# A two-layer encoder's 256-token matmul stages: the high weights take the high and the low activations in one 512-column matmul

## The chip, the cores and the metric

One core of one Trainium2 chip. The metric is the time of one execution on the device in microseconds (us), the median of three runs. PE is the matrix engine (TensorE), PEld its weight load, DVE the vector engine, ACT the scalar engine, POOL the GpSimd engine, SP the engine whose queue issues nearly all loads.

## The reference

Two layers of an encoder, each a mixer and a SwiGLU feed-forward network (FFN), each of these wrapped as x <- LayerNorm(alpha x + f(x)). Layer 0 mixes with a diagonal state space and latent attention, layer 1 with a Mamba-2 scan. All is float32. In front of the 256 tokens stand 16 meta tokens; their positions are dropped at the end, so from the z part of layer 1's mixer on only 256 tokens are needed.

```python
D_MODEL = 2048
BATCH = 1
SEQ = 256
...
def mamba2_mixer(h, w_in, conv_w, conv_b, dt_bias, a_log, d, norm_g, w_out):
    bsz, n, _ = h.shape
    zxbcdt = h @ w_in
    z = zxbcdt[..., :SSD_INNER]
...
    y = y.reshape(bsz, n, SSD_INNER) * jax.nn.silu(z)
...
    return y @ w_out

def swiglu_ffn(h, w_gate, w_up, w_down):
    return (jax.nn.silu(h @ w_gate) * (h @ w_up)) @ w_down
```

## The kernel before, in words

Activations lie with features on partitions and tokens on columns. Every matrix product goes through `linear` (L135): it walks a list SEQ[name] of weight tiles (m, k) of 128 x 128, row tile m after row tile m, and adds the products over k into one PSUM tile of 512 float32 columns (one bank) per m. Float32 is kept by splitting: a weight tile is high + low, an activation tile high + low, each part in the type float32r, and three matmuls (L162 to L164) make high x high, high weights x low activations and low weights x high activations, all into the same 256 or 272 columns. The high and the low activations are two tiles (hh and hl for a layer's input, ah and al for the FFN's hidden features, yh and yl for the output of the scan).

The weights come in loads of eight tiles on SP's queue (L121, four buffers). ACT casts a load to its high part (L126) and DVE subtracts (L127) to make the low part; three buffers hold the pairs. In the input projection and the output projections of layer 1 both work in halves of 512 columns. When the last k of a row tile is done, `evac` reads PSUM: in the FFN silu on ACT for a gate tile (m < 44), a product on DVE for an up tile, then a split; in the down product an addition to x on DVE; for z (m < 32 of the input projection) silu on ACT; in the output projection an addition to x on DVE. Four PSUM tiles take turns as accumulators in these stages.

The stages of layer 1 with 256 tokens: the z tiles of the input projection (in1_0 to in1_7, which the trace calls mm_in; between them stand tiles with 272 tokens for the scan), the output projection in three parts (out1a, out1b, out1c: 16, 8 and 8 tiles k for each of the 16 m), and the FFN (gate and up in gu_a and gu_b, down in dn_a and dn_b; here with a 1 behind the name for layer 1, which the trace leaves out and whose input it calls m1hh, m1hl). In out1c and dn_b `ln_add` (L282) adds the last part to x and goes on to the sums of the layer norm; gu_a1 takes its first seven row tiles before the norm is known, with two more columns (258), and corrects them afterwards.

A scheduler that simulates the program sets the order of the instructions on each engine; each engine then runs its list strictly in order.

Of the kernel before, what the change touches and what calls it, by code (L numbers as in the profile page):

```python
# [8 lines left out]
F32 = mybir.dt.float32  # L9
F32R = mybir.dt.float32r  # L10
# [8 lines left out]
N = 272          # tokens with the meta tokens  # L19
NM = 16          # meta tokens  # L20
NS = 256         # tokens without them
D = 2048
DT = 16          # feature tiles of the model width
KC = 8           # weight tiles per load
# [4 lines left out]
NHT = 44         # hidden tiles of the FFN  # L29
HH = 22          # hidden tiles of one half  # L30


# ---------------------------------------------------------------- orders
def seq_rows(ms, ks, first=0):
    """Order of the weight tiles (m, k): the first `first` row tiles interleaved
    over k, the others one after the other."""
    s = [(m, k) for k in ks for m in ms[:first]]
    for m in ms[first:]:
        s += [(m, k) for k in ks]
    return s  # L40


# the tiles after a layer norm, in the order in which its results come
KS = list(range(8, 16)) + list(range(8))
PRE = (3, 1, 1, 2)  # groups of the row tiles that take the sums before the norm
# [41 lines left out]
# vectors by feature: name -> (first column, columns)  # L87
# [12 lines left out]
# ---------------------------------------------------------------- kernel  # L100
class Trunk:
# [9 lines left out]
    # ---- weights: load, split exactly into two parts of 12 bits each  # L111
# [23 lines left out]
    def linear(self, name, rhs, evac, n, pre=None):  # L135
        """rhs(k, m) -> (hi, lo) [128, n]; n may be a function of m. pre: (norm, tile), with
        the first row tiles taken before the norm and corrected after it."""
# [9 lines left out]
        for i, (m, k) in enumerate(seq):  # L147
# [6 lines left out]
            if m in before:  # L154
                nn += 2
                o = ps[m][:, :nn]
                xh, xl = rhs(k, m, 2)
            else:
                xh, xl = rhs(k, m)
            st = left[m] == tot[m]  # L160
            left[m] -= 1
            nc.tensor.matmul(o, lhsT=wh, rhs=xh, start=st, stop=False)  # L162
            nc.tensor.matmul(o, lhsT=wh, rhs=xl, start=False, stop=False)  # L163
            nc.tensor.matmul(o, lhsT=wl, rhs=xh, start=False, stop=left[m] == 0)  # L164
            if left[m] == 0:
                del ps[m]
# [16 lines left out]

    def split(self, hi, lo, src):
# [3 lines left out]
    # ---- sums over features, token by token: (tokens of a tile) on partitions, tiles on columns  # L188
# [4 lines left out]
    def colsum(self, o, terms, ones, n):  # L193
        """o [tokens, tiles] = sum over partitions of the terms [128, n], times the value of ones"""
# [8 lines left out]
    def spread(self, pool, ps, r, n):  # L203
        """r [tokens, tiles] to all partitions, [128, n] in PSUM"""
# [10 lines left out]
    def rsqrt(self, pool, v, n, act, e=None):  # L215
        """1 / sqrt(v), v [tokens, tiles] in SBUF, >= eps > 0; Newton steps after a first guess"""
# [21 lines left out]
    def rms(self, pool, ps, sq, w, n, e=None):  # L238
        """1 / sqrt(mean of squares + eps), to all partitions in PSUM; sq: sums of squares by partition"""
# [12 lines left out]
    # ---- layer norm over features (partitions and tiles), token by token.  # L252
    # x is kept as x - K, K the mean over the first feature tile, and the sums are taken of that.
    # Up to the first row tiles of the next matrix W, g (x - K) goes for the result:
    #   W (g (x - mean) r + b) = r (W g (x - K)) - (mean - K) r (W g) + W b,
    # with g and b as two more columns.
    def ln_begin(self, pool, ps, xs, g=None, b=None, hh=None, hl=None, late=0, tag=None):
        n = xs[0].shape[-1]
        if hh is not None:
            for j, v in ((N, g), (N + 1, b)):  # L260
                v = self.vecs[:, VEC[v][0]:VEC[v][0] + DT]
                self.split(hh[:, :, j], hl[:, :, j], v)
        return dict(pool=pool, ps=ps, xs=xs, n=n, g=g, b=b, hh=hh, hl=hl, late=late, tag=tag)
# [1083 lines left out]
```

## Time and profile before

| | |
|---|---|
| time, median of 3 runs | 2723.07 us (2720.76 to 2724.64) |
| span of the profiled execution | 2719.2 us |
| PE busy | 2654.8 us (98%), 21808 matmuls |
| DVE busy | 1680.2 us (62%) |
| ACT busy | 1275.6 us (47%) |
| POOL busy | 421.6 us (16%) |
| loads | mean 171 GB/s |

The span runs from the first to the last instruction of the one profiled execution; the timed runs are other executions of the same program, and what they take beyond the span lies before its first instruction and after its last. Busy times are averages over stages with different limits. PE's records are pipelined and overlap, so its busy share says that something is always in it, and the distance from one start to the next says how fast it goes. In layer 1, gu_a1 begins at 1929 us, dn_a1 at 2191, gu_b1 at 2318 and dn_b1 at 2569; out1a lies from 1619 to 1709, out1b from 1820 to 1879 and out1c from 1879 to 1929.

### The profile page before, as it was taken

To read this page: it belongs to the slowest core of one execution; us is meant where nothing else is said; L and a number is where in the kernel's file an instruction comes from. 1 tells how busy PE (TensorE), PEld (TensorE's weight loads), DVE (VectorE), ACT (ScalarE), POOL (GpSimd) and SP (SyncE) were. 2 spreads that over 40 slices of the span, in tenths; PEclk is the share of its full clock that TensorE was granted. 3 is DMA by queue.
4 is the path that set the end of the run, shared out by engine and by line. 5 is a ranking of instruction groups with operands and counts; after the bars stand their busy time and mean duration, and the time that the engine had idled before them with its cause. 6 is when DMAs were issued, how large, how long until landed. Compare 5 with 4: busy or idle time off the path is not lost.

```text
span 2719.2 us, 52890 instructions
## 1 busy us (share of the span) xinstructions
PE 2654.8 (98%) x21808; PEld 2600.5 (96%) x21808; DVE 1680.2 (62%) x2692; ACT 1275.6 (47%) x2040; POOL 421.6 (16%) x576
## 2 busy tenths in 40 slices
PE   9899999999999999999999999999899999999997
PEld 8677999999999999999999999999899999999997
DVE  7768587444444445669677775788964444444555
ACT  5545456333333334447555554555654433444443
POOL 5844061000000001220001110113500000000042
PEclk9899999999999999999999999999999999999999
DMA  7233545555555555545655555554556556565663
GB/s 244 84 109 103 187 155 158 176 171 176 175 177 172 175 174 172 178 151 180 209 158 191 179 175 189 173 162 144 187 189 183 184 185 184 183 185 185 186 180 116
DMA packets 139682, 465.30 MB, mean 171 GB/s; under 512 B 14832, under 2 KB 30000, under 8 KB 139312
## 3 DMA queue, kind: packets, MB, share of 16 engines
q1 hardware_dynamic: 139296, 461.71, 54.5%
q8 instruction: 171, 2.80, 0.4%
q14 instruction: 71, 0.58, 0.1%
q10 hardware_dynamic: 144, 0.21, 0.0%
HBM read 458.58 MB, written 3.28 MB: 170 GB/s over the span
## 4 chain that ended last, share of the span: by engine, by line
PE 88%; DVE 6%; POOL 3%; issue 1%; ACT 1%; DMA 1%; SPq 0%; DVEq 0%; ACTq 0%; POOLq 0%
PE mm_gu_b L164 6%; PE mm_gu_b L163 6%; PE mm_gu_b L162 6%; PE mm_gu_a L164 6%; PE mm_gu_a L162 6%; PE mm_gu_a L163 6%; PE mm_in L163 5%; PE mm_in L162 5%; PE mm_in L164 5%; PE mm_dn_b L162 3%; PE mm_dn_a L162 3%; PE mm_dn_b L164 3%; PE mm_dn_b L163 3%; PE mm_dn_a L164 3%; PE mm_dn_a L163 3%
## 5 line engine op out<-in xcount | busy, mean ns | idle before, releaser
L127 DVE TENSOR_TENSOR lo_gu_b<-st_gu_b,hi_gu_b 128x1024 fp32r<-128x1024 f32 x176 | 215.7, 1226 | 235.6 <-ACT hi_gu_b L126 235.6
L127 DVE TENSOR_TENSOR lo_gu_a<-st_gu_a,hi_gu_a 128x1024 fp32r<-128x1024 f32 x176 | 216.3, 1230 | 188.3 <-ACT hi_gu_a L126 186.8
L126 ACT CAST hi_gu_b<-st_gu_b 128x1024 fp32r<-128x1024 f32 x176 | 184.9, 1050 | 308.5 <-PE mm_gu_b L163 226.6
L126 ACT CAST hi_gu_a<-st_gu_a 128x1024 fp32r<-128x1024 f32 x176 | 184.4, 1048 | 251.4 <-PE mm_gu_a L163 190.4
L163 PE MATMUL mm_in<-f0hl,hi_in 128*128 128x256 f32 (+1 forms) x1024 | 293.2, 287 | 0.0
L162 PE MATMUL mm_in<-f0hh,hi_in 128*128 128x256 f32 (+1 forms) x1024 | 292.6, 286 | 0.0
L164 PE MATMUL mm_in<-f0hh,lo_in 128*128 128x256 f32 (+1 forms) x1024 | 292.5, 286 | 0.0
L304 POOL TENSOR_TENSOR x<-x,ln_k 128x272 f32<-128x272 f32 (+1 forms) x56 | 60.1, 1111 | 1396.6 <-ACT ln_k L302 1298.2
L127 DVE TENSOR_TENSOR lo_in<-st_in,hi_in 128x512 fp32r<-128x512 f32 (+1 forms) x268 | 183.4, 716 | 96.4 <-ACT hi_in L126 95.6
L126 ACT CAST hi_in<-st_in 128x512 fp32r<-128x512 f32 (+1 forms) x268 | 158.3, 636 | 148.0 <-PE mm_in L163 135.3
L164 PE MATMUL mm_gu_a<-mixhh,lo_gu_a 128*128 128x272 f32 (+1 forms) x704 | 203.7, 291 | 3.5 <-DVE lo_gu_a L127 3.5
L162 PE MATMUL mm_gu_a<-mixhh,hi_gu_a 128*128 128x272 f32 (+1 forms) x704 | 204.0, 290 | 1.1 <-DVE fix L276 1.1
L163 PE MATMUL mm_gu_a<-mixhl,hi_gu_a 128*128 128x272 f32 (+1 forms) x704 | 204.3, 291 | 0.0
L163 PE MATMUL mm_gu_b<-mixhl,hi_gu_b 128*128 128x272 f32 x704 | 203.5, 289 | 0.0
L164 PE MATMUL mm_gu_b<-mixhh,lo_gu_b 128*128 128x272 f32 x704 | 203.5, 289 | 0.0
L162 PE MATMUL mm_gu_b<-mixhh,hi_gu_b 128*128 128x272 f32 x704 | 203.4, 289 | 0.0
L164 PE MATMUL mm_gu_a<-m1hh,lo_gu_a 128*128 128x256 f32 (+1 forms) x704 | 198.5, 283 | 4.9 <-DVE lo_gu_a L127 4.9
L162 PE MATMUL mm_dn_b<-ah,hi_dn_b 128*128 128x272 f32 (+1 forms) x704 | 201.1, 286 | 0.0
L164 PE MATMUL mm_dn_b<-ah,lo_dn_b 128*128 128x272 f32 (+1 forms) x704 | 201.1, 286 | 0.0
L163 PE MATMUL mm_dn_b<-al,hi_dn_b 128*128 128x272 f32 (+1 forms) x704 | 201.0, 286 | 0.0
L162 PE MATMUL mm_dn_a<-ah,hi_dn_a 128*128 128x272 f32 (+1 forms) x704 | 201.0, 286 | 0.0
L164 PE MATMUL mm_dn_a<-ah,lo_dn_a 128*128 128x272 f32 (+1 forms) x704 | 200.9, 285 | 0.0
(519 smaller groups left out, 8886.4 us busy)
## 6 DMA issues: line engine op xcount, KB each, us to landing
st_gu_a<-in_w_gu_a SPq DMA_DIRECT2D x176, 512.0 KB, 3.6
st_gu_b<-in_w_gu_b SPq DMA_DIRECT2D x176, 512.0 KB, 3.6
st_in<-in_w_in SPq DMA_DIRECT2D x140, 512.0 KB, 3.7
st_dn_a<-in_w_dn_a SPq DMA_DIRECT2D x88, 512.0 KB, 3.5
st_dn_b<-in_w_dn_b SPq DMA_DIRECT2D x88, 512.0 KB, 3.5
st_in1h<-in_w_in1h SPq DMA_DIRECT2D x34, 512.0 KB, 3.6
st_out1a<-in_w_out1a SPq DMA_DIRECT2D x32, 512.0 KB, 3.6
st_out0b<-in_w_out0b SPq DMA_DIRECT2D x16, 512.0 KB, 3.9
```

The costliest lines, as they stand in the source:

```text
L126: nc.scalar.copy(hi[:, j:j + w], st[:, j:j + w])
L127: nc.vector.tensor_tensor(lo[:, j:j + w], st[:, j:j + w], hi[:, j:j + w], op=ALU.subtract)
L162: nc.tensor.matmul(o, lhsT=wh, rhs=xh, start=st, stop=False)
L163: nc.tensor.matmul(o, lhsT=wh, rhs=xl, start=False, stop=False)
L164: nc.tensor.matmul(o, lhsT=wl, rhs=xh, start=False, stop=left[m] == 0)
L304: (nc.vector if j < 2 else nc.gpsimd).tensor_tensor(xs[j], xs[j], st["k"], op=ALU.subtract)
```

## The change

High and low activations of a tile lie in one tile now, side by side ([128, k, 2, tokens]: hx, ax, yx). Where a matmul has exactly 256 columns, `linear` sends the high weights against both halves in one instruction of 2 x 256 columns, which fills the 512 columns of the PSUM tile; the low weights go against the high half and into the first 256 columns as before. A row tile thus ends as two partial sums, p and q, which `evac` adds: where silu or a product follows, a new helper `merged` copies q with ACT and adds p with DVE; where x is added to, DVE adds p and then q. Products with 258, 260, 272 or 274 columns keep their three matmuls. The FFN's silu tiles get a fifth buffer. The operands of layer 0 get the same layout. All else in the diff is names and removed comments.

```diff
...
             if m in before:
                 nn += 2
                 o = ps[m][:, :nn]
-                xh, xl = rhs(k, m, 2)
+                x2 = rhs(k, m, 2)
             else:
-                xh, xl = rhs(k, m)
+                x2 = rhs(k, m)
+            xh, xl = x2[:, 0, :], x2[:, 1, :]
             st = left[m] == tot[m]
             left[m] -= 1
-            nc.tensor.matmul(o, lhsT=wh, rhs=xh, start=st, stop=False)
-            nc.tensor.matmul(o, lhsT=wh, rhs=xl, start=False, stop=False)
-            nc.tensor.matmul(o, lhsT=wl, rhs=xh, start=False, stop=left[m] == 0)
+            if nn == NS:
+                nc.tensor.matmul(ps[m].rearrange("p (a b) -> p a b", a=2), lhsT=wh, rhs=x2, start=st, stop=False)
+                nc.tensor.matmul(o, lhsT=wl, rhs=xh, start=False, stop=left[m] == 0)
+            else:
+                nc.tensor.matmul(o, lhsT=wh, rhs=xh, start=st, stop=False)
+                nc.tensor.matmul(o, lhsT=wh, rhs=xl, start=False, stop=False)
+                nc.tensor.matmul(o, lhsT=wl, rhs=xh, start=False, stop=left[m] == 0)
             if left[m] == 0:
-                del ps[m]
+                t = ps.pop(m)
+                if nn == NS:
+                    evac(m, o, t[:, NS:])
+                    continue
                 if m not in before:
                     evac(m, o)
                     continue
...
                 if not groups:
                     self.ln_split(pre[0])
 
+    def merged(self, t, p, q):
+        if q is None:
+            return p
+        self.nc.scalar.copy(t, q)
+        self.nc.vector.tensor_tensor(t, t, p, op=ALU.add)
+        return t
...
-    def ln_add(self, st, i, p):
+    def ln_add(self, st, i, p, q=None):
         nc, pool, n, xs = self.nc, st["pool"], st["n"], st["xs"]
         x = xs[i]
-        nc.vector.tensor_tensor(x, x, p, op=ALU.add)
+        for a in (p, q):
+            if a is not None:
+                nc.vector.tensor_tensor(x, x, a, op=ALU.add)
         self.ln_sums(st, i, x)
...
     def operand(self, name):
-        return (self.res.tile([P, DT, N + 2], F32R, tag=t, name=name + t) for t in ("hh", "hl"))
+        return self.res.tile([P, DT, 2, N + 2], F32R, tag="hx", name=name)
...
             for half in range(2):
-                ah = pool.tile([P, HH, n], F32R, tag="ah", name=f"ah{layer}{half}")
-                al = pool.tile([P, HH, n], F32R, tag="al", name=f"al{layer}{half}")
+                ax = pool.tile([P, HH, 2, n], F32R, tag="ax", name=f"ax{layer}{half}")
                 hold = {}
 
-                def evac(m, p):
+                def evac(m, p, q=None):
+                    s = pool.tile([P, n], F32, tag="silu", bufs=5, name="silu")
                     if m < NHT:
-                        s = hold[m] = pool.tile([P, n], F32, tag="silu", bufs=4, name="silu")
-                        nc.scalar.activation(s, p, AF.Silu)
+                        hold[m] = s
+                        nc.scalar.activation(s, self.merged(s, p, q), AF.Silu)
                         return
                     j = m - NHT
+                    p = self.merged(s, p, q)
                     s = hold.pop(j)
                     nc.vector.tensor_tensor(s, s, p, op=ALU.mult)
-                    self.split(ah[:, j - half * HH, :], al[:, j - half * HH, :], s)
+                    self.split(ax[:, j - half * HH, 0, :], ax[:, j - half * HH, 1, :], s)
 
...
                 def rhs_d(k, m):
-                    return ah[:, k - half * HH, :], al[:, k - half * HH, :]
-                def evac_d(m, p):
+                    return ax[:, k - half * HH, :, :]
+                def evac_d(m, p, q=None):
                     if half == 0:
                         nc.vector.scalar_tensor_tensor(xs[m], xs[m], ALPHA, p, op0=ALU.mult, op1=ALU.add)
+                        if q is not None:
+                            nc.vector.tensor_tensor(xs[m], xs[m], q, op=ALU.add)
                     else:
-                        self.ln_add(st2, m, p)
+                        self.ln_add(st2, m, p, q)
...
             def proj(g):
-                def evac(m, p):
+                def evac(m, p, q=None):
                     if m < 32:
                         z = pool.tile([P, NS], F32, tag="z", bufs=8, name="z")
-                        nc.scalar.activation(z, p, AF.Silu)
+                        nc.scalar.activation(z, self.merged(z, p, q), AF.Silu)
                         z_t[m] = z
...
             def wout(name, ks, first, final):
-                def evac(m, p):
+                def evac(m, p, q):
+                    if final:
+                        self.ln_add(st, m, p, q)
+                        return
                     if first:
                         nc.vector.scalar_tensor_tensor(xl[m], xl[m], ALPHA, p, op0=ALU.mult, op1=ALU.add)
-                    elif final:
-                        self.ln_add(st, m, p)
                     else:
                         nc.vector.tensor_tensor(xl[m], xl[m], p, op=ALU.add)
+                    nc.vector.tensor_tensor(xl[m], xl[m], q, op=ALU.add)
 
                 def yr(k, m):
-                    yh, yl = ys[k // 4]
-                    return yh[:, k % 4, :], yl[:, k % 4, :]
+                    return ys[k // 4][:, k % 4]
...
+        yx = ys[g] = pool.tile([P, 4, 2, NS], F32R, tag="yx", bufs=4, name="yx")
         r = self.rms(pool, ps, [tot], 512, NS, nc.gpsimd)
         for j in range(4):
             nc.vector.scalar_tensor_tensor(yf[j], yf[j], self.vec("ssd_g", 4 * g + j), r, op0=ALU.mult, op1=ALU.mult)
-            self.split(yh[:, j, :], yl[:, j, :], yf[j])
+            self.split(yx[:, j, 0, :], yx[:, j, 1, :], yf[j])
```

The scheduler's order on DVE at three places. First, the end of the input projection (the z tiles 28 to 31 of in1_7) and the first weights of out1b; lo_x is the low part of a load, mm_x the accumulator. Before:

```order
L186 TENSOR_TENSOR yl<-z,yh 128x256 x4
L127 TENSOR_TENSOR lo_in_7_13_21193<-st_in_7_13_21190,hi_in_7_13_21192 128x512 x2
L127 TENSOR_TENSOR lo_in_7_14_21227<-st_in_7_14_21224,hi_in_7_14_21226 128x512 x2
L127 TENSOR_TENSOR lo_in_7_15_21260<-st_in_7_15_21257,hi_in_7_15_21259 128x512 x2
L127 TENSOR_TENSOR lo_out1b_21596<-st_out1b_21593,hi_out1b_21595 128x512 x2
```

and now:

```order
L198 TENSOR_TENSOR z<-z,mm_in_7_28_20432 128x256
L127 TENSOR_TENSOR lo_in_7_14_20586<-st_in_7_14_20583,hi_in_7_14_20585 128x512 x2
L198 TENSOR_TENSOR z<-z,mm_in_7_29_20485 128x256
L127 TENSOR_TENSOR lo_in_7_15_20611<-st_in_7_15_20608,hi_in_7_15_20610 128x512 x2
L127 TENSOR_TENSOR lo_out1b_20939<-st_out1b_20936,hi_out1b_20938 128x512 x2
L198 TENSOR_TENSOR z<-z,mm_in_7_30_20538 128x256
```

Each z tile's accumulator is now read by DVE between two splits. Second, the beginning of out1b, ahead of a long run of scan work (y, z, de). Before:

```order
L809 TENSOR_TENSOR x_3477<-x_3477,mm_out1b_21601 128x256
L127 TENSOR_TENSOR lo_out1b_21698<-st_out1b_21695,hi_out1b_21697 128x512 x2
L809 TENSOR_TENSOR x_3477<-x_3477,mm_out1b_21635 128x256
L127 TENSOR_TENSOR lo_out1b_21732<-st_out1b_21729,hi_out1b_21731 128x512 x2
L925 SCALAR_TENSOR_TENSOR y<-xs,vecs,y_p 128x256 x2
```

and now:

```order
L831 TENSOR_TENSOR x_3475<-x_3475,mm_out1b_20944 128x256
L127 TENSOR_TENSOR lo_out1b_21020<-st_out1b_21017,hi_out1b_21019 128x512 x2
L831 TENSOR_TENSOR x_3475<-x_3475,mm_out1b_20971 128x256
L127 TENSOR_TENSOR lo_out1b_21047<-st_out1b_21044,hi_out1b_21046 128x512 x2
L832 TENSOR_TENSOR x_3475<-x_3475,mm_out1b_20944 128x256
L832 TENSOR_TENSOR x_3475<-x_3475,mm_out1b_20971 128x256
```

The second halves of the first two row tiles (L832) stand behind two more loads' splits and ahead of the scan's y. Third, the middle of out1c, where m1hl (now m) is the next matrix's operand, ln_s the sums of the norm. Before:

```order
L269 SCALAR_TENSOR_TENSOR m1hl<-x_3477,vecs,m1hh 128x256
L285 TENSOR_TENSOR x_3477<-x_3477,mm_out1c_22450 128x256
L313 TENSOR_TENSOR ln_s_22180<-ln_s_22180,x_3477 128x256
L127 TENSOR_TENSOR lo_out1c_22565<-st_out1c_22562,hi_out1c_22564 128x512 x2
L269 SCALAR_TENSOR_TENSOR m1hl<-x_3477,vecs,m1hh 128x256
L313 TENSOR_TENSOR ln_s_22180<-ln_s_22180,x_3477 128x256
L285 TENSOR_TENSOR x_3477<-x_3477,mm_out1c_22490 128x256
L127 TENSOR_TENSOR lo_out1c_22605<-st_out1c_22602,hi_out1c_22604 128x512 x2
```

and now:

```order
L304 TENSOR_TENSOR x_3475<-x_3475,mm_out1c_21631 128x256
L286 SCALAR_TENSOR_TENSOR m_21368<-x_3475,vecs,m_21368 128x256
L304 TENSOR_TENSOR x_3475<-x_3475,mm_out1c_21664 128x256
L127 TENSOR_TENSOR lo_out1c_21758<-st_out1c_21755,hi_out1c_21757 128x512 x2
L332 TENSOR_TENSOR ln_s_21403<-ln_s_21403,x_3475 128x256
L304 TENSOR_TENSOR x_3475<-x_3475,mm_out1c_21664 128x256
L286 SCALAR_TENSOR_TENSOR m_21368<-x_3475,vecs,m_21368 128x256
L304 TENSOR_TENSOR x_3475<-x_3475,mm_out1c_21697 128x256
L127 TENSOR_TENSOR lo_out1c_21791<-st_out1c_21788,hi_out1c_21790 128x512 x2
L304 TENSOR_TENSOR x_3475<-x_3475,mm_out1c_21697 128x256
```

Every row tile has two additions from its accumulator (L304) where it had one (L285), with a split or a sum between them.

## Rows read from the trace of the kernel before

**Rows 1.** The page, its head and part 1: busy time by engine.

```profile
span 2719.2 us, 52890 instructions
...
PE 2654.8 (98%) x21808; PEld 2600.5 (96%) x21808; DVE 1680.2 (62%) x2692; ACT 1275.6 (47%) x2040; POOL 421.6 (16%) x576
```

**Rows 2.** The page, part 4: chain that ended last, by engine.

```profile
PE 88%; DVE 6%; POOL 3%; issue 1%; ACT 1%; DMA 1%; SPq 0%; DVEq 0%; ACTq 0%; POOLq 0%
```

**Rows 3.** Windows: us, then busy us (records) of PE, PEld, DVE, ACT, POOL; clock; DMA; GB/s.

```profile
2400.00:2500.00 100.00, 100.00 (x843) 100.00 (x843) 49.36 (x53) 41.73 (x52) 0.00 (x0) 1.00 0.60 184
2210.00:2310.00 100.00, 100.00 (x836) 100.00 (x835) 46.91 (x47) 36.30 (x35) 0.00 (x0) 1.00 0.60 183
...
1630.00:1700.00 70.00, 70.00 (x599) 70.00 (x599) 37.84 (x63) 28.54 (x50) 0.00 (x0) 1.00 0.60 189
900.00:1000.00 100.00, 100.00 (x792) 100.00 (x792) 46.61 (x50) 39.58 (x49) 0.00 (x0) 1.00 0.55 173
680.00:780.00 100.00, 100.00 (x801) 100.00 (x800) 45.81 (x47) 34.67 (x33) 0.00 (x0) 1.00 0.58 175
```

**Rows 4.** Timeline of PE at the vp matmuls (start, us), and vp among the groups by form.

```profile
121.51 1.88 PE L607 MATMUL vp<-wv,kvl 128*80 128x512 f32 x4
...
L607 PE MATMUL vp<-wv,kvl 128*128 128x512 f32 x8 | 3.6, 592 | 0.0
```

**Rows 5.** Groups by line and form, PE, whole span: xcount | busy us, mean ns.

```profile
L164 PE MATMUL mm_gu_b<-m1hh,lo_gu_b 128*128 128x256 f32 x704 | 198.2, 282 | 0.0
...
L164 PE MATMUL mm_gu_a<-m1hh,lo_gu_a 128*128 128x256 f32 x592 | 166.4, 282 | 0.0
...
L164 PE MATMUL mm_in<-f0hh,lo_in 128*128 128x256 f32 x512 | 145.4, 284 | 0.0
...
L164 PE MATMUL mm_dn_a<-ah,lo_dn_a 128*128 128x256 f32 x352 | 99.6, 283 | 0.0
...
L164 PE MATMUL mm_out1a<-yh,lo_out1a 128*128 128x256 f32 x256 | 71.6, 280 | 0.0
...
L164 PE MATMUL mm_out1b<-yh,lo_out1b 128*128 128x256 f32 x128 | 36.1, 285 | 0.0
```

**Rows 6.** Groups by line, ACT, 1879 to 1930 us.

```profile
L302 ACT COPY ln_k<-ln_kp 128x256 f32<-128x256 f32 x1 | 0.4, 362 | 0.0
```

**Rows 7.** What PE waited for, 1800 us to the end: us in total, times, longest us.

```profile
PE mm_gu_a L164 <- DVE lo_gu_a L127: 4.9, 3, 3.1
PE mm_out1c L164 <- DVE lo_out1c L127: 2.3, 4, 1.0
```

**Rows 8.** Timelines of DVE and PE in out1b and out1c: start us, us, instruction, [idle before].

```profile
1840.35 0.40 DVE L809 TENSOR_TENSOR x<-x,mm_out1b 128x256 f32<-128x256 f32 x1
1840.67 0.68 DVE L127 TENSOR_TENSOR lo_out1b<-st_out1b,hi_out1b 128x512 fp32r<-128x512 f32 x1
...
1841.64 0.28 PE L164 MATMUL mm_out1b<-yh,lo_out1b 128*128 128x256 f32 x1
...
1917.78 0.38 PE L164 MATMUL mm_out1c<-yh,lo_out1c 128*128 128x256 f32 x1 [0.97 <-DVE lo_out1c L127]
```

**Rows 9.** Windows, as rows 3: input projection, gu_b1, then out1b and out1c in four pieces.

```profile
1305.80:1618.80 313.00, 312.81 (x2594) 304.74 (x2593) 230.07 (x490) 174.36 (x326) 34.22 (x60) 1.00 0.57 181
...
2317.90:2569.00 251.10, 251.10 (x2113) 251.10 (x2113) 124.18 (x131) 105.00 (x131) 0.00 (x0) 1.00 0.59 185
...
1820.20:1841.40 21.20, 21.20 (x190) 19.27 (x189) 20.36 (x55) 10.42 (x17) 3.16 (x3) 1.00 0.25 77
1841.40:1879.20 37.80, 37.19 (x326) 35.64 (x325) 32.83 (x70) 16.41 (x34) 9.58 (x27) 1.00 0.55 168
1879.20:1900.20 21.00, 20.54 (x172) 20.29 (x171) 17.48 (x30) 11.84 (x26) 10.98 (x12) 1.00 0.45 151
1900.20:1930.20 30.00, 27.48 (x216) 26.00 (x216) 29.69 (x43) 16.70 (x35) 22.35 (x22) 1.00 0.50 157
```

**Rows 10.** Timeline of DVE at the end of dn_b1.

```profile
2698.19 0.42 DVE L285 TENSOR_TENSOR x<-x,mm_dn_b 128x256 f32<-128x256 f32 x1 [7.79 <-PE mm_dn_b L164]
```

## What I expected of the change, before it ran

> **What bounds the kernel now.** I read the engine table first: PE is busy 2654.8 of 2719.2 us and DVE 1680.2 [rows 1]; then the chain of work that ended last, which runs 88% on PE and 6% on DVE [rows 2]. So the time is, nearly everywhere, the matmul count times the spacing of matmuls. A busy PE is not a PE at its peak, so the next view is that spacing: windows that lie wholly inside one stage, with the number of PE records [rows 3]. A record lasts 0.28 us (0.29 at 272 columns; [rows 5]) and they start about 0.12 us apart, so some 2.4 (2.3) of the counted ones began before the window. In the 256-token stages this gives 100 us / 840.6 = 118.9 ns (gate/up), 100 / 833.6 = 120.0 ns (down) and 70 / 596.6 = 117.3 ns (out1a); in the 272-token stages 100 / 789.7 = 126.6 ns and 100 / 798.7 = 125.2 ns. The granted clock is 1.00 in all five, the upper level of 2.4 GHz. At one column per clock 256 columns are 106.7 ns and 272 are 113.3 ns. So every matmul carries 12.2, 13.3, 10.7, 13.3 and 11.9 ns beyond its columns. What the change is worth hangs on whom this excess belongs to: the instruction or its columns.
>
> **Whose the excess is.** If it were the columns', 16 more of them would add 256 to 272 in proportion: 7.4 to 7.5 ns. Gate/up adds 126.6 - 118.9 = 7.7, down adds 125.2 - 120.0 = 5.2; the mean, 6.4, is 0.40 ns a column, beside 0.417 at 2.4 GHz. So the two pairs together say: per instruction, about 12 ns; the gate/up pair alone would say: per column. Sixteen columns are a short lever, and I keep both readings. A third reading comes from the only 512-column matmuls, vp in plain float32 [rows 4]: four records take 1.88 us, a record is 0.59 long, so three spacings of 0.429 us, which is twice 512 columns (426.7 ns) and under 3 ns more. They take a column in two clocks, so they don't show what a fast long matmul pays, only that a long slow one pays almost nothing.
>
> The Trainium skill speaks against the change here: TensorE: Matmul & The Clock Gate, section "Back-to-back issue gap", gives N / 2.4 + 2.5 ns for an N-column matmul, and its Part 2 says that loading the next weights takes no read bandwidth from the running one. This case's spacing of 118.9 ns stands 9.7 ns over that formula's 109.2. By the formula alone a merged pair would save 2.5 ns and the whole change 3024 x 2.5 = 7.6 us; by the rows it is 10.7 to 13.3 each.
>
> **The change part by part.** (1) *Matmuls.* Each weight tile of a 256-column stage goes from 256 + 256 + 256 columns in three instructions to 512 + 256 in two, with one weight load fewer. The tiles are 704 in gu_b1, 592 in gu_a1 (its first seven row tiles stay at 258 columns and three instructions), 352 each in dn_a1 and dn_b1, 512 in the z part of the input projection, 256 in out1a, 128 each in out1b and out1c [rows 5]. If the excess is the instruction's, one excess goes per tile: gate/up 1296 x 12.2 = 15.8 us, z 512 x 12.2 = 6.2 (the same operand layout; taken from gate/up, since z alternates with 272-column tiles), down 704 x 13.3 = 9.4, out1a 256 x 10.7 = 2.7. Sum 34.1 us. Out1b and out1c would give another 256 x 11 = 2.8, which I count as nothing, for the reason in (3).
>
> (2) *ACT.* 113 more copies of the low half (81 silu, 32 z). The nearest row is the copy of 128x256 out of PSUM, 0.36 us [rows 6]. In gu_b1 that is 44 x 0.36 = 16 us on an engine busy 105 of 251; no price. The banks are held longer, but four take turns and one row tile lasts 16 x 0.36 = 5.7 us; the list of what PE waits for between 1800 us and the end has no eviction in it; its two longest lines are the splits [rows 7].
>
> (3) *DVE.* 193 more additions of 128x256, one operand in PSUM: 44 + 37 silu, 32 z, 16 in each of dn_a1, dn_b1, out1a, out1b, out1c. The row is the addition of x in out1b: 0.40 us long, and the next instruction starts 0.32 after it [rows 8]. In gu_b1 DVE goes from 124 to 124 + 44 x 0.40 = 142 us of a stage of 242 [rows 9]: covered. Out1a and the two down stages stay under two thirds [rows 3]. In the input projection DVE is busy 230 of 313 us [rows 9] and gets 20 x 0.40 = 8 more: covered by the mean, with a rival below. The cover is gone from out1b to the first gate/up tiles. Four windows that follow on each other [rows 9] show DVE busy 20.36 of 21.2, 32.83 of 37.8, 17.48 of 21.0 and 29.69 of 30.0 us. At 1841.64 PE starts on a low half whose split ended 0.3 us before, at 1840.67 + 0.68; and from 1900 it starts each low half when the split releases it, as at 1917.78 after 0.97 us idle [rows 8]. Step by step, from the order: before the split at 1841.35 stand six new additions (the z tiles 28 to 31, two of out1b): 6 x 0.32 = 1.9, less the lead of 0.3, a stall of 1.6 us. Between there and 1900 stand 18 (14 of out1b, 4 of out1c): 5.8 to 7.2 us against 8.5 us in which DVE was idle in the two windows (37.8 - 32.8 and 21.0 - 17.5); I take 0, and 5.8 as the upper bound. From 1900 to 1930 ten, with no idle time: 3.2 to 4.0, I take 3.6. Behind the first gate/up split two, 0.6 us: PE is waiting for these very splits (4.9 us in three waits [rows 7]). Sum 5.8 us, bounds 4 to 12. A PE that is faster there only waits longer, hence the zero in (1). ACT, which casts the high half ahead of each split, is busy 45 of these 89 us (16.4 + 11.8 + 16.7) and is not what comes next.
>
> (4) *The end.* The last row tile of dn_b1 has two dependent additions where it had one of 0.42 us, alone on the path [rows 10]: 0.4 us.
>
> (5) *No price:* the operands' new layout moves no instruction, SP issues the same loads (907 rows of order before and now), and the first layer has the same matmuls, with 272 columns throughout.
>
> Sum: -34.1 + 5.8 + 0.4 = -27.9 us on the span of 2719.2. The median of the three runs is 2723.07, so 3.9 us lie around the span. 2719.2 - 27.9 + 3.9 = 2695.2 us.
>
> **The rivals.** *A. The excess is the columns'.* For it: the gate/up pair (7.7 ns for 16 columns); against it: the down pair (5.2). Then 512 columns cost as two times 256, nothing is saved, and only the price of DVE's additions from 1841 us on is left, with the end: +6.2 us, 2719.2 + 6.2 + 3.9 = 2729.3, slower. It decides as soon as a merged pair saves under 6.2 us / 2768 tiles = 2.2 ns. *A'.* The same, but a small part is the instruction's, the 2.7 ns that vp shows over its columns: 2768 x 2.7 = 7.5 us back, 2721.8, no change. It would be the outcome by the formula of the Trainium skill named above (TensorE: Matmul & The Clock Gate). *B. A long matmul hides what a short one pays,* as vp does: then the 512-column one keeps 2.7 ns of its excess too. Further gain: (1296 + 512) x 9.5 + 704 x 10.6 + 256 x 8.0 = 26.7 us, 2668.5. Against it: vp runs at half the rate. *C. DVE's queue holds the splits up.* The additions wait for a copy on ACT, which waits for PE's last matmul of the row tile, and behind them on DVE stand the splits of the next weights. In the z parts that can cost 8 groups x about 1 us: 2703.2. Against it: DVE is idle a quarter of that stretch, and PE waits for no split there. *D. It doesn't do what it says:* excluded by the order: in these stages, and in no others, a 512- and a 256-column matmul stand where three of 256 stood, 3024 instructions fewer.
>
> **How the numbers follow.** Forecast 0.66, with bounds of its own from 10.7 to 13.3 ns a tile (29.6 to 36.8 us) and 4 to 12 us on DVE: 2690 to 2706. B 0.10, C 0.08, A' 0.07, A 0.09. Faster by over 0.2%, about what a measurement here can tell from no change (5.4 us), holds for the forecast, B and C: 0.84; within 0.2% is A', 0.07; slower is A, 0.09. The range takes in the forecast, C and A' (0.81) and part of the way to B: 2680 to 2724.
>
> **What would show it.** In gu_b1 a weight tile, now 3 x 118.9 = 357 ns, takes 344.5 by the forecast, 334.9 by B, about 354 by A' and 357 by A; in dn_a1 346.7 instead of 360. From 1841 on, shifted by what was saved earlier, the list of PE's waits should hold lo_out1b, lo_out1c and lo_gu_a with some 14 us together instead of 7, and DVE should be busy over 95% in out1c. If PE's waits are no longer there, step (3) is wrong; if the tile time is not near 344, step (1).

## The result: 2707.4 us, and the profile after

| | before | after |
|---|---|---|
| median (range), us | 2723.2 (2720.8 to 2724.6) | 2707.4 (2705.9 to 2710.2) |
| ratio to before | | 0.9939, 95% interval 0.9922 to 0.9956 |
| span of the profiled execution, us | 2719.2 | 2708.3 |

The change is faster by 15.8 us; the forecast was 27.9. The page of the changed kernel, its head and the busy times, to be held against [rows 1]:

```profile
span 2708.3 us, 47222 instructions
...
PE 2636.8 (97%) x18784; PEld 2446.4 (90%) x18784; DVE 1750.0 (65%) x2885; ACT 1311.2 (48%) x2153; POOL 424.7 (16%) x576
```

3024 matmuls are gone, 193 DVE and 113 ACT instructions are new, as the order said. The windows of [rows 3] again (us, then busy us and records of PE, PEld, DVE, ACT, POOL; clock; DMA share; GB/s): gate/up, down and out1a, then gate/up and down of the first layer.

```profile
2400.00:2500.00 100.00, 100.00 (x573) 87.40 (x572) 56.40 (x72) 47.60 (x71) 0.00 (x0) 1.00 0.60 188
2210.00:2310.00 100.00, 100.00 (x568) 86.68 (x567) 53.01 (x62) 37.40 (x36) 0.00 (x0) 1.00 0.59 187
1630.00:1700.00 70.00, 70.00 (x406) 61.63 (x405) 41.44 (x75) 28.62 (x51) 0.00 (x0) 1.00 0.60 189
900.00:1000.00 100.00, 100.00 (x798) 100.00 (x797) 47.37 (x50) 39.83 (x50) 0.00 (x0) 1.00 0.56 176
680.00:780.00 100.00, 100.00 (x798) 100.00 (x798) 45.75 (x46) 34.60 (x33) 0.00 (x0) 1.00 0.56 176
```

Two records make a weight tile now; they last 0.395 and 0.28 us, so 1.9 of the counted ones began before the window. A tile takes 100 / ((573 - 1.9) / 2) = 0.3502 us in gate/up, 353.3 ns in down and 346.4 in out1a. The forecast had 344.5 and 346.7 for the first two; before it was 357 and 360. The last two lines show stages whose matmuls are the same as before: 798 records where [rows 3] has 792 in gate/up and 801 in down.

What PE waited for from 1800 us on (us in total, times, longest), beside [rows 7]:

```profile
PE mm_gu_a L170 <- DVE lo_gu_a L127: 5.7, 3, 4.3
PE mm_out1c L165 <- DVE x L304: 3.4, 2, 3.1
PE y_p L941 <- DVE de L924: 1.7, 1, 1.7
PE ln_c L216 <- DVE x L304: 1.1, 1, 1.1
PE mm_out1c L166 <- DVE lo_out1c L127: 1.0, 2, 0.7
PE y_p L941 <- DVE de L922: 0.9, 1, 0.9
PE mm_out1b L166 <- DVE lo_out1b L127: 0.8, 1, 0.8
```

Two more lines of the same list before the change:

```profile
PE mm_gu_a L162 <- DVE x L285: 0.8, 1, 0.8
PE y_p L920 <- DVE de L903: 0.6, 1, 0.6
```

In out1c the wait for L304 is new. L304 is the addition from the accumulator, so the first matmul of a row tile waits for its bank (an accumulator's place in PSUM). Nearly all of it is one wait (start us, us, instruction, [idle before]):

```profile
1896.42 0.47 PE L165 MATMUL mm_out1c<-yx,hi_out1c 128*128 128x512 f32 x1 [3.12 <-DVE x L304]
```

And out1b and out1c as windows:

```profile
1816.50:1877.00 60.50, 57.04 (x384) 48.26 (x382) 57.63 (x135) 26.20 (x48) 14.35 (x28) 1.00 0.40 130
1877.00:1931.00 54.00, 48.76 (x260) 40.80 (x260) 50.17 (x87) 28.45 (x60) 31.70 (x35) 0.97 0.44 141
```

The timelines give the length of each stage, from its first matmul's start to that of the next stage (for dn_b1 to the start of its own last one; "z to end" goes to the end of the span; us; the kernels behind "after" are explained below):

| kernel | z to out1b | out1b, out1c | gu_a1 | dn_a1 | gu_b1 | dn_b1 | z to end |
|---|---|---|---|---|---|---|---|
| before | 514.4 | 109.2 | 261.8 | 126.7 | 251.2 | 128.8 | 1413.4 |
| after | 511.2 | 114.6 | 258.9 | 124.1 | 246.7 | 126.1 | 1403.0 |
| layout_only | 513.9 | 109.2 | 261.3 | 126.7 | 250.5 | 128.8 | 1411.7 |
| first_half | 513.2 | 111.3 | 258.1 | 122.0 | 246.8 | 124.5 | 1396.8 |
| hybrid | 511.2 | 109.4 | 258.2 | 124.1 | 246.7 | 126.1 | 1397.1 |
| ordered | 511.2 | 114.6 | 258.9 | 122.0 | 246.8 | 124.5 | 1399.4 |
| hybrid_ordered | 511.3 | 109.4 | 258.1 | 122.0 | 246.8 | 124.5 | 1393.5 |
| all_three | 511.2 | 111.0 | 258.4 | 124.4 | 248.7 | 124.5 | 1399.7 |

A second execution of the changed kernel (after_again, below) has the stages of the first to 0.1 us, while its z began at 1301.0 us instead of 1305.3. The differences in this table are therefore worth more than those of whole runs.

### The profile page after: what moved, and what is told of

It is laid out like the page before. It is cut to its first block, busy times and chain, and to the rows that moved or that the text cites. A ratio compares the mean times of both kernels' runs of the same rounds, so it can differ in the third digit from the quotient of the medians.

```text
span 2708.3 us, 47222 instructions
## 1 busy us (share of the span) xinstructions
PE 2636.8 (97%) x18784; PEld 2446.4 (90%) x18784; DVE 1750.0 (65%) x2885; ACT 1311.2 (48%) x2153; POOL 424.7 (16%) x576
## 4 chain that ended last, share of the span: by engine, by line
PE 87%; DVE 6%; POOL 4%; ACT 1%; issue 1%; DMA 0%; DVEq 0%; ACTq 0%; POOLq 0%
PE mm_gu_b L165 6%; PE mm_gu_a L165 5%; PE mm_in L165 4%; PE mm_gu_a L170 4%; PE mm_gu_a L168 4%; PE mm_gu_a L169 4%; PE mm_gu_b L170 3%; PE mm_gu_b L168 3%; PE mm_gu_b L169 3%; PE mm_gu_b L166 3%; PE mm_dn_b L165 3%; PE mm_dn_a L165 3%; PE mm_gu_a L166 3%; PE mm_in L166 2%; PE mm_in L169 2%; PE mm_in L170 2%
## 5 line engine op out<-in xcount | busy, mean ns | idle before, releaser
L165 PE MATMUL mm_gu_b<-m,hi_gu_b 128*128 128x512 f32 x704 | 246.8, 395 | 0.0
L165 PE MATMUL mm_gu_a<-m,hi_gu_a 128*128 128x512 f32 x592 | 207.5, 395 | 0.0
L170 PE MATMUL mm_gu_a<-mix,lo_gu_a 128*128 128x272 f32 (+1 forms) x704 | 203.8, 291 | 3.6 <-DVE lo_gu_a L127 3.6
L168 PE MATMUL mm_gu_a<-mix,hi_gu_a 128*128 128x272 f32 (+1 forms) x704 | 203.8, 290 | 1.1 <-DVE fix L293 1.1
L169 PE MATMUL mm_gu_a<-mix,hi_gu_a 128*128 128x272 f32 (+1 forms) x704 | 204.3, 291 | 0.0
L170 PE MATMUL mm_gu_b<-mix,lo_gu_b 128*128 128x272 f32 x704 | 203.2, 289 | 0.0
L169 PE MATMUL mm_gu_b<-mix,hi_gu_b 128*128 128x272 f32 x704 | 202.7, 288 | 0.0
L168 PE MATMUL mm_gu_b<-mix,hi_gu_b 128*128 128x272 f32 x704 | 202.5, 288 | 0.0
L166 PE MATMUL mm_gu_b<-m,lo_gu_b 128*128 128x256 f32 x704 | 197.2, 280 | 0.0
L165 PE MATMUL mm_in<-f,hi_in 128*128 128x512 f32 x512 | 180.6, 396 | 0.0
L166 PE MATMUL mm_gu_a<-m,lo_gu_a 128*128 128x256 f32 x592 | 165.6, 280 | 0.0
L165 PEld LDWEIGHTS mm_gu_b<-m,hi_gu_b 128*128 128x128 f32 x704 | 132.5, 188 | 31.2
```

The costliest lines, as they stand in the source:

```text
L165: nc.tensor.matmul(ps[m].rearrange("p (a b) -> p a b", a=2), lhsT=wh, rhs=x2, start=st, stop=False)
```

## The experiments

Each is an edit of the changed kernel unless said otherwise. The kernel before took 2722.6, 2722.4, 2724.3 and 2727.1 us (medians) beside the four groups of runs, so ratios to it are compared.

**The layout alone.** `linear` goes back to three matmuls, and `evac` gets no second half; hx, ax, yx and the fifth silu buffer stay.

```diff
-            if nn == NS:
+            if False:
...
-                    evac(m, o, t[:, NS:])
+                    evac(m, o, None)
...
```

> The side-by-side layout stays, but every 256-column tile goes back to three matmuls of 256 columns and one addition at eviction. Theory 1 (the saving comes from the merged instruction, the layout gives only the 2 us seen in the 272-column stage gu_b0): gu_b1 at 357 ns a weight tile, dn_b1 at 360, about 2721 us. Rival (the layout is what makes matmuls cheaper everywhere): gu_b1 near 351 ns and dn_b1 near 353, 2707 to 2712 us.

Measured: 2714.8 us, ratio 0.9970 (0.9959 to 0.9982). Its windows in gate/up, out1a and the first layer's gate/up:

```profile
2400.00:2500.00 100.00, 100.00 (x845) 100.00 (x844) 49.69 (x53) 41.73 (x52) 0.00 (x0) 1.00 0.59 185
1630.00:1700.00 70.00, 70.00 (x593) 70.00 (x592) 37.47 (x63) 28.58 (x50) 0.00 (x0) 1.00 0.62 187
900.00:1000.00 100.00, 100.00 (x798) 100.00 (x798) 47.74 (x51) 39.89 (x50) 0.00 (x0) 1.00 0.55 176
```

Gate/up is hardly touched (845 records, 843 before), out1a is slower (593, 599 before), the first layer's gate/up faster (798, 792). From the first matmul of the first layer's second gate/up half to its down half it takes 265.2 us instead of 267.2, and the first half 274.5 instead of 276.4. So neither side was right in full: the merged instruction is what shortens the 256-token stages (gu_b1 250.5 us and dn_b1 128.8, as theory 1 has them), but the layout alone moves matmuls of the same size both ways, and about half of the change's gain comes with it. The stages account for some 5 of its 7.8 us: 3.9 in the first layer's gate/up, less 0.4 in each of its down halves, and 1.7 from z to the end. The rest is in no stage that this run shows.

**The second half not read.** The merged tiles' `evac` gets the first half alone:

```diff
-                    evac(m, o, t[:, NS:])
+                    evac(m, o, None)
...
```

> The merged matmuls stay, but the second half of the PSUM tile is never read: the high weights times the low activations are computed and left out of the result, and with them 193 additions on VectorE and 113 copies on ScalarE. Theory 1 (the additions cost the 5.4 us that out1b to the head of gu_a1 lost): 2701 to 2703 us, and TensorE's waits on the eviction line in out1c are gone. Rival (those waits come from the order of the weight splits, not from the additions): within 1 us of the changed kernel, 2706 to 2708 us.

Measured: 2703.2 us, ratio 0.9925 (0.9909 to 0.9940), as theory 1 has it, but from two places, and against 2.0 us more from z to out1b, for which no run shows a reason. Out1b and out1c take 111.3 us, 3.3 less than after and still 2.1 more than before; its list of waits, from 1800 us on, shows where:

```profile
PE mm_gu_a L170 <- DVE lo_gu_a L127: 5.1, 3, 3.1
PE mm_out1c L166 <- DVE lo_out1c L127: 3.5, 6, 1.0
...
PE mm_out1c L165 <- DVE x L304: 0.2, 1, 0.2
```

The wait for the bank is gone (3.4 to 0.2), but PE meets DVE's splits more often (6 times, 3.5 us; 4 and 2.3 in [rows 7]). The other place is not on DVE at all: dn_a1 takes 122.0 us instead of 124.1, and dn_b1 124.5 instead of 126.1, where its matmuls wait for nothing.

```profile
2210.00:2310.00 100.00, 100.00 (x579) 88.15 (x578) 48.70 (x49) 37.98 (x36) 0.00 (x0) 1.00 0.60 189
```

579 records are 346.6 ns a tile, and the forecast was 346.7.

**Three matmuls in out1b and out1c alone.** `evac` gets no second half there.

```diff
-            if nn == NS:
+            if nn == NS and name not in ("out1b", "out1c"):
...
```

> out1b and out1c alone go back to three matmuls and one addition; z, out1a and the FFN stay merged. Theory 1 (the second additions are paid only where VectorE is the bound): out1b plus out1c take 113 us as before the change rather than 115, the head of gu_a1 starts some 5 us earlier relative to out1b, 2702 us in all. Rival (the head of gu_a1 pays because its own weight splits and evictions are behind, whatever out1c does): 2705 to 2707 us.

Measured: 2703.0 us, ratio 0.9920 (0.9906 to 0.9934); out1b and out1c take 109.4 us again (before it was 109.2, and not the 113 of the expectation), and gu_a1 0.7 less than after.

```profile
1815.70:1874.90 59.20, 58.46 (x513) 54.85 (x511) 53.53 (x125) 27.17 (x50) 11.78 (x30) 1.00 0.41 135
1874.90:1925.10 50.20, 47.70 (x388) 46.19 (x387) 46.43 (x71) 27.72 (x61) 32.39 (x33) 1.00 0.45 152
```

Theory 1 holds.

**Half of the low weights' load.** In gu_b1 and dn_b1, for all k but the last (P is 128):

```diff
-                nc.tensor.matmul(o, lhsT=wl, rhs=xh, start=False, stop=left[m] == 0)
+                c = P // 2 if name in ("gu_b1", "dn_b1") and left[m] else P
+                nc.tensor.matmul(o[:c], lhsT=wl[:, :c], rhs=xh, start=False, stop=left[m] == 0)
```

> In gu_b1 and dn_b1 the low weights of all k but a row tile's last are loaded with 64 of their 128 columns and multiply into 64 of 128 output rows; the product for the other rows is left out. The streamed columns (512 + 256 a tile) are the same. Theory L (what a matmul takes beyond its columns comes with the weight load that runs beside it): the distance from a 512-column start to the next falls from 234 towards 223 ns, gu_b1 from 247 to about 239 us, dn_b1 from 126 to 122 us, some 11 us less in all. Theory C (it goes with the streamed columns or is a fixed amount per instruction): gu_b1 stays at 246 to 247 us and the total at that of the changed kernel.

Measured, in one execution: gu_b1 247.0 us. Its line, and that of the changed kernel:

```profile
2312.70:2559.70 247.00, 247.00 (x1410) 180.51 (x1409) 138.85 (x175) 117.35 (x174) 0.00 (x0) 1.00 0.59 188
2314.10:2560.80 246.70, 246.70 (x1410) 215.54 (x1409) 138.92 (x175) 117.28 (x174) 0.00 (x0) 1.00 0.60 188
```

PEld is busy 180.5 us instead of 215.5 of the stage, and the stage is as long. Theory L falls for gu_b1: the time beyond the columns does not shrink with the low weights' load. (The Trainium skill, TensorE: Matmul & The Clock Gate, Part 2, has the next weights read through a port of their own; the 247.0 us agree with that.) Dn_b1 came to 124.0 us, though, which neither theory has; the next run shows what kind of difference that is.

**PE's order in the down stages.** What differs in dn_a1 between first_half and the changed kernel? PE's timeline of the latter shows matmuls that stand the wrong way round (start us, us), of which first_half has none in its down stages:

```profile
2197.99 0.39 PE L165 MATMUL mm_dn_a<-ax,hi_dn_a 128*128 128x512 f32 x1
2198.22 0.28 PE L166 MATMUL mm_dn_a<-ax,lo_dn_a 128*128 128x256 f32 x1
2198.33 0.39 PE L165 MATMUL mm_dn_a<-ax,hi_dn_a 128*128 128x512 f32 x1
2198.56 0.28 PE L166 MATMUL mm_dn_a<-ax,lo_dn_a 128*128 128x256 f32 x1
2198.68 0.63 PE L165 MATMUL mm_dn_a<-ax,hi_dn_a 128*128 128x512 f32 x2
2199.14 0.40 PE L166 MATMUL mm_dn_a<-ax,lo_dn_a 128*128 128x256 f32 x2
```

Two high ones in a row, then two low ones (x2). A row tile has 22 weight tiles here, and this is the 26th of the stage: in the order that the scheduler set, the last tile of row tile 0 stands between the two matmuls of a tile of row tile 1. Up to there tiles start 0.347 us apart. At 2203.9 follows a second such place, the first high matmul of row tile 2 among the last four tiles of row tile 1; behind it tiles take 353 ns, to the end of the stage. The edit binds the order of dn_a1 and dn_b1 without a wait (a and b are the two matmuls of a tile):

```diff
+INROW = ('dn_a1', 'dn_b1')
...
+                if name in INROW:
+                    if prev is not None:
+                        self.behind(a, prev)
+                    self.behind(b, a)
+                    prev = b
...
```

> The changed kernel with one addition: in dn_a1 and dn_b1 TensorE's matmuls are bound to stand in the order of the program, so that a row tile's last matmul is never placed behind the first of the next. In the changed kernel, where two such places stand at 2199 and 2204 us, the weight tile goes from 346.7 to 353.3 ns there and stays at that. Theory 1 (the exchanged pair puts the matmuls out of a rhythm that then does not come back by itself): dn_a1 352 x 346.7 = 122.0 us instead of 124.1, dn_b1 some 2 us less, the total some 4 us below the changed kernel, about 2703 us. Rival (the second additions, which begin at the same place, disturb TensorE by their reads of PSUM): 353.3 ns and 2707 us.

Measured: 2705.2 us, ratio 0.9929 (0.9908 to 0.9951). The ratio's interval covers the changed kernel's 0.9939, so the total decides nothing; the stage does:

```profile
2190.10:2312.10 122.00, 122.00 (x707) 107.56 (x705) 66.19 (x77) 46.98 (x46) 0.00 (x0) 1.00 0.58 190
```

122.0 / 352 = 346.6 ns, with both additions in place, so they do not disturb PE. Theory 1 holds. The pair has two rhythms in the down stages, 346.7 and 353.3 ns, and keeps the one it is in until something shifts it. In dn_b1 that is also the layer norm's float32 matmul ln_kp: ordered begins the stage at 353 ns and goes on at 346.7 behind ln_kp, at 2571.5 us. Half_low's dn_b1 is another case: its timeline has 346.5 ns from the first tiles on, and about 347 behind the three exchanged places at 2568.4, 2573.9 and 2582.3 us, where the changed kernel ends at 353.3. So the low weights' load may have a part in the rhythm; no run separates that.

**Where the columns lie.** Three kernels, of one execution each, ask why gate/up has neither rhythm but 350 ns; their edits stand here in words. First, aligned rows for the normed input (a view of the same tile):

```diff
-        hx: rows of N + 2 = 274, tokens from column 16 on
+        hx: rows of 272, tokens from column 0 on
```

> The changed kernel, but the input of layer 1's FFN lies in rows of 272 columns with the 256 tokens first, not in rows of 274 with the tokens behind 16 unused columns; the low half now starts 1088 bytes behind the high half. gu_a1 and gu_b1 read it. Theory 1 (what the gate and up tiles take beyond the forecast, 350.5 against 344.5 ns, is due to where the rows start): 345 to 347 ns, gu_b1 about 243.5 us instead of 246.7. Rival (the gap between the halves is what costs, wherever the rows start): 350 to 351 ns.

```profile
2400.00:2500.00 100.00, 100.00 (x574) 87.56 (x573) 56.52 (x72) 47.93 (x72) 0.00 (x0) 1.00 0.59 189
```

349.6 ns: theory 1 falls. Second, with and without a gap, the down stages in bound order; j is the tile k, f the operand as one row:

```diff
+    gu_b1:  f[:, 516 * j:516 * j + 512]
+    dn_a1:  f[:, 512 * j:512 * j + 548] as 2 x 274, of each the first 256
+    dn_b1:  f[:, 512 * j + 16:512 * j + 528]
```

> A look at distances alone: layer 1's FFN reads wrong columns, so its result is left out. gu_a1: rows of 258, the halves 2 columns apart. gu_b1: 512 columns without a gap. dn_a1: 2 x 256 columns with a gap of 18 between them. dn_b1: 512 without a gap, starting 16 columns late; both down stages in the order of the program. Theory 1 (a gap between the halves costs 4 ns a tile): gu_b1 346.7 ns a tile and dn_b1 346.7, gu_a1 and dn_a1 350 to 351. Rival (it goes by the weights' order in the stage, so that gate and up pay it and down does not): gu_b1 350.5, dn_a1 346.7.

```profile
2210.00:2300.00 90.00, 90.00 (x521) 78.57 (x520) 47.93 (x56) 34.33 (x33) 0.00 (x0) 1.00 0.58 188
2400.00:2500.00 100.00, 100.00 (x569) 87.08 (x569) 55.87 (x72) 47.61 (x71) 0.00 (x0) 1.00 0.58 185
2580.00:2660.00 80.00, 80.00 (x460) 70.07 (x459) 47.96 (x55) 33.69 (x40) 24.83 (x22) 1.00 0.58 190
```

Down with a gap takes 346.8 ns, gate/up without one 352.7: the gap is not it, and the rival comes near. (Dn_a1 began at 353 ns here and changed at 2200 us with its order bound, so an exchanged place is not the only thing that shifts the rhythm.) Dn_b1, 64 bytes later, took 349.3. Third, tile k 2048 bytes behind tile k - 1, as in ax and yx:

```diff
+    gu_b1:  f[:, 512 * j:512 * j + 512]
+    gu_a1:  f[:, 512 * j + 16:512 * j + 528]
```

> A look at distances alone: layer 1's FFN reads wrong columns, so its result is left out. All tiles of gu_b1 and the merged ones of gu_a1 read 512 columns without a gap and with one tile k 2048 bytes behind the other, as down and out1a do; in gu_a1 the first column lies 64 bytes later. Theory 1 (the rhythm goes by where a tile's columns start: with starts that repeat every 2048 bytes the pair keeps to 346.7 ns): gu_b1 704 x 346.7 = 244.1 us instead of 246.7, gu_a1 within 3 ns of 346.7. Rival (gate and up are slower for another reason, such as the weights' order or the splits beside them): 350 to 352 ns and 246.6 to 247.8 us.

```profile
2318.20:2562.20 244.00, 244.00 (x1410) 213.31 (x1409) 138.95 (x175) 117.30 (x174) 0.00 (x0) 1.00 0.59 190
```

244.0 / 704 = 346.6 ns, and 349 in gu_a1 with its shift of 64 bytes: as theory 1 has it, and against the weights' order as the reason. (The total, 2709.6, is no measure: gu_a1 waited for rows that it does not need.)

**Fewer columns in the merged matmul.**

```diff
+                c = NS if st else COLS.get(name, NS)
-    ... rhs=x2, ...
+    ... rhs=x2[:, :, :c], ...
```

> The merged matmul takes fewer tokens of each half for all k of a row tile but the first, and the rest is left out: 2 x 128 in gu_a1, 2 x 192 in dn_a1, 2 x 224 in gu_b1, 2 x 240 in dn_b1. The weight loads and the number of matmuls stay. Theory F (a fixed amount per matmul, 20.7 ns for the merged one): the distance from its start to the next is columns/2.4 plus 20 to 21 ns everywhere: 127 ns at 256 columns, 207 at 448. Theory C (part of it goes with the columns, 0.027 ns each, and 5.5 ns with the instruction): 119 ns at 256 columns, 204 at 448.

Windows in gu_a1 (2 x 128), dn_a1 (2 x 192) and gu_b1 (2 x 224):

```profile
2000.00:2100.00 100.00, 100.00 (x816) 98.93 (x815) 80.83 (x104) 69.59 (x103) 0.00 (x0) 1.00 0.82 271
2130.00:2230.00 100.00, 100.00 (x678) 99.34 (x677) 64.25 (x76) 44.47 (x43) 0.00 (x0) 1.00 0.72 224
2300.00:2400.00 100.00, 100.00 (x614) 94.10 (x613) 60.48 (x77) 50.90 (x76) 0.00 (x0) 1.00 0.63 202
```

The first matmul of a row tile has 512 columns, so a pair has 528, 646 and 708 columns on average: 220.0, 269.1 and 295.0 ns at 2.4 GHz. The tiles take 245.8, 295.9 and 326.7, that is 25.8, 26.8 and 31.7 ns more, beside 30.2 (gate/up) and 26.6 (down in the shorter rhythm) at 768. The theories speak of one distance alone, from a merged matmul's start to the next. On the timelines it is 119.5 ns on average behind 256 columns, 176.1 behind 384 and 206.1 behind 448. So theory F falls (127 at 256 columns), and theory C's 119 comes out; at 448 the value lies between C's 204 and F's 207.

C's slope does not hold in down, though: there the merged matmul takes 16.1 ns beyond 384 columns and 16.7 beyond 512, the low one behind it 10.9 and 10.0 beyond its 256. In down a pair's excess is thus 26.6 to 27 ns whatever its width, where three matmuls of 256 had 40: the prediction's reading, a fixed amount per instruction, holds there for the sum (13.3 ns each on average), but the two do not share it evenly. In gate/up the excess wanders from 25.8 to 31.7 ns.

**Both gains together**, and the changed kernel beside it:

> Three matmuls in out1b and out1c, merged ones elsewhere, and the down stages' matmuls in the order of the program. Theory 1 (the two gains are in different stages and add up): some 4.4 us from out1b to the head of gu_a1 and 3.5 to 4 us in dn_a1 and dn_b1 below the changed kernel, 2698 to 2700 us. Rival (one takes away what the other gave, since a faster stage brings its evictions and weight splits closer together): 2702 to 2704 us.

> The changed kernel once more, on the chip and in the rounds of the kernel that stands beside it. Every theory: its time of before, 2706 to 2710 us, so that the difference between the two is that of one chip.

Measured: 2699.4 us, ratio 0.9909 (0.9896 to 0.9923), and 2707.9, ratio 0.9946 (0.9932 to 0.9959). The intervals do not meet: it is 8.5 us faster than the change as made and 24.9 faster than before. Theory 1 holds (z to end 1393.5 us, 9.5 less than after).

**And gate/up in rows of 2048 bytes.** The rows of the seven tiles before the norm keep 258 columns.

> As hybrid_ordered, and layer 1's FFN reads its normed input from rows of 512 columns, one tile k 2048 bytes behind the other (the rows of the seven tiles before the norm keep their two further columns, 258 a half). Theory 1 (starts that repeat every 2048 bytes hold the pair at 346.7 ns in gate and up too): gu_b1 244.0 us instead of 246.7, gu_a1 some 2 us less, about 2694 to 2696 us in all. Rival (the writing over of the rows in another stride makes the first normed tiles wait for the last ones before the norm, and takes it back): gu_b1 244.0 us but gu_a1 2 us or more longer, 2698 to 2700 us.

Measured: 2707.4 us, ratio 0.9930 (0.9917 to 0.9942), its z to end is 6.2 us longer than hybrid_ordered's, and by neither theory: gu_a1 is not 2 us longer, but gu_b1 takes 248.7 and dn_a1, with its order bound, 124.4. (Out1b and out1c take 1.6 us more, too.)

```profile
2308.20:2556.90 248.70, 248.70 (x1409) 215.75 (x1409) 138.89 (x175) 117.36 (x174) 0.00 (x0) 1.00 0.57 186
2183.80:2308.20 124.40, 124.40 (x707) 107.83 (x706) 66.26 (x77) 46.75 (x46) 0.00 (x0) 1.00 0.58 186
```

248.7 / 704 = 353.3 ns. In gu_a1, whose order is not bound, three exchanged pairs stand at 1978.6, 1982.9 and 1988.8 us; behind them the tiles go at 353.3, and this is carried through dn_a1 and gu_b1 up to ln_kp in dn_b1. Regular starts thus keep a rhythm, be it the shorter or the longer one. That binding gu_a1's order as well would give 346.7 there was not run and stays open.

## Why the prediction was right, and where not

The time lies in the range, 12 us above the forecast and 1.4 above the forecast's own bounds. It lies there in part by luck: one term was 18 us too large, and one that was left out brought some 8 (of which 1.7 lie from z to the end). From z to the end the steps gave -34.1 + 5.8 + 0.4 = -27.9 us; the table gives -15.9 + 5.4 + 0.1 = -10.4.

1. **Term (1) was mis-sized by half**: 3.2 (z and out1a) + 2.9 + 2.6 + 4.5 + 2.7 = 15.9 us instead of 34.1, and by layout_only 1.7 of these come with the layout. The step that failed is "one excess goes per tile", with the other two left as they were. The tile times of the change as made do not decide between the rivals: 350 ns in gate/up lies nearer to A' (354) than to the forecast (344.5; A had 357, B 334.9), and 353 in down halfway between A's 360 and the forecast's 346.7. It is the later runs that speak for the instruction. In down, ordered reaches 346.6, and the exchanged pairs had cost 6.7 ns of the 13.3. In gate/up, stride reaches 346.6 with other starts; as made, a pair carries 30.2 ns there, so 6.5 of 12.2 are saved. That the 12.2 was a mean over columns that start at changing places fits the timeline of before (115 to 123 ns from start to start in gate/up, 120 throughout in down), but it is argued and not shown. A spacing of equal matmuls does not tell that of unequal ones. As to A': the section of the Trainium skill that the prediction names for it (TensorE: Matmul & The Clock Gate, "Back-to-back issue gap") calls its formula the gap of an isolated matmul and has other figures for streams of load and matmul, so it does not speak against the change as the prediction says. No run comes near its 131 ns for 512 columns in such a stream either; the shortest mean distance behind 512 columns is 229.2 ns (out1a).
2. **Term (3) was right in size** (5.4 for 5.8 us), but not step by step, and DVE is busy 93% of out1c, where over 95% was forecast. The three split lines together were to grow from 7 to some 14 us and stayed at 7.5 (5.7 + 1.0 + 0.8): lo_out1c fell to 1.0, and 3.4 went to banks that waited for an addition. The longest of these waits (3.1 us) lies in the stretch that was taken at 0. "The list has no eviction in it" was a misreading of before: mm_gu_a waited 0.8 us for x L285, the addition out of the accumulator; and the change doubles the additions. First_half splits the 5.4: 3.3 for the second additions, and 2.1 that stay with the merged matmuls alone. Whether a faster PE or the scheduler's other order makes these 2.1 is not shown.
3. **Term (5), the layout at no price, was wrong**: alone it gave 7.8 us of the median (ratio 0.9970, so 5 to 11), of which 3.9 us are seen in the first layer's gate/up (2.5 in the profile of after). The edit leaves the matmuls as they are, but moves where their columns start, and the spacing of equal matmuls changed with it (792 to 798 records in 100 us). That the starts are the reason is argued from gate/up in layer 1; the edit moves other tiles, too.
4. **Rival C**, DVE's queue holding the splits up in the z parts, did not come: PE waits for no split there, only 1.7 us for POOL (rms_c), where it was 0.2. Something like it happened in out1b: y_p waits for DVE's de 2.6 us in two waits, where it was 0.6 before. Term (2), ACT at no price, held: the list has no wait for ACT. The end, (4), cost 0.1.
5. The 3.9 us "around the span" are in fact 1.9 (2710.16 timed, 2708.3 span), so the profiled run of before was probably near the shortest of its three (2720.76); since the sum started from the median all the same, this cost nothing.

## What to carry to other kernels

Merge matmuls where PE is the bound, and leave them as they are in a stage that the evicting engine bounds: the merge saved 6.5 ns a tile in gate/up and cost 5.4 us in out1b and out1c. Behind a merge into unequal matmuls read PE's timeline around the row tiles' edges; exchanged pairs there cost 2.1 us in dn_a1, and PE's list of waits shows nothing of it. And a price per instruction read from one spacing is to be given as a range that takes in half of it, until a run with the new sizes has been seen.

## What the runs showed of the hardware

- A 512-column and a 256-column float32r matmul in turn, with tiles 2048 bytes apart, take 346.7 ns (16.7 and 10.0 beyond columns / 2.4) or 353.3, by what went before, with the same instructions and operands and a granted clock of 1.00 (dn_a1 of ordered and of after). The state outlasts hundreds of pairs (all_three: all of gu_b1). Why is not settled. Half the low weights' load did not shorten gu_b1 (247.0 us), but dn_b1 kept about 347 ns with it.
- Equal matmuls of 272 columns went from 126.6 to 125.6 ns with the layout's edit alone (792 and 798 records in 100 us of gate/up); for 256 columns out1a shows the opposite sign (599 and 593 in 70).
- The first layer's clock scatters between executions: the same matmuls (out0b) took 54 us in hybrid and 60 in hybrid_ordered, at a granted clock of 1.00 and 0.89, and PE waited for 0.7 us at most in either:

```profile
255.00:311.00 56.00, 56.00 (x490) 54.69 (x489) 34.23 (x55) 24.33 (x40) 0.00 (x0) 1.00 0.51 172
255.00:316.00 61.00, 61.00 (x486) 59.32 (x485) 34.78 (x56) 24.31 (x40) 0.00 (x0) 0.89 0.47 158
```
